# The first modulation read in eight pieces, S5's parameters moved behind it, and five reads on another queue

## The chip, the cores and the metric

One core of a Trainium2 chip runs the whole program. Its engines are TensorE (PE; PEld is its weight load), VectorE (DVE), ScalarE (ACT) and GpSimd (POOL); SyncE (SP) issues transfers, and so do ACT and POOL on queues of their own. The metric is the device time of one execution in microseconds; lower is better.

## What is computed

The reference is a trunk of two layers on 512 latent and 256 context tokens of width 1024. What matters here is the start of layer 0:

```python
mod = jax.nn.silu(c) @ w_mod + b_mod            # [1024] @ [1024, 6144], for c and for c_ctx
sh1, sc1, ... = jnp.split(mod, 6)
proj = (x * (1.0 + sc1) + sh1) @ w_in           # the operand of the projection, then the projection
pr, ps, pq, pk, pv = jnp.split(proj, ...)       # inputs of RWKV, S5 and attention
# S5: a complex state space model; its parameters come from lam_re, lam_im and log_dt
dt = jnp.exp(log_dt)[:, None]
mag = jnp.exp(lam_re * dt)
ab_re, ab_im = mag * jnp.cos(lam_im * dt), mag * jnp.sin(lam_im * dt)
```

Behind it follow the three mixers, the output product, a mixture of 32 experts, and the second layer in the same way.

## The kernel before, in words

`trunk` (L2099) runs the stages in order; the change touches the first stage of layer 0 (L2124 to L2152), and the next one, `input_side` (L2055), takes over its results.

**First stage.** `mod_c` (L91) reads `c` and `c_ctx`, applies silu, and reads `b_mod` in columns. `s5_params` (L1001) computes the table `s_pk` (powers of the discretised states, for both layers and directions) out of three small parameters. Its five reads go out on ACT's queue (L1010, L1015); two transposes bring lambda to the layout needed (L1017), and some 150 VectorE instructions, nearly all on 128 x 64 elements, do the rest; at the end `s_pk` is stored by SP (L1093). `win` (L214) reads a 256-column piece of `w_in` and splits it into two float32r parts (ACT L225, VectorE L226). `mod_unit` (L114) takes `n` columns of `w_mod`: a read on SP (L118), 16 matmul pieces for the 8 row groups (L127), an eviction on ACT (L129), small matmuls that fold and transpose it (L135), and an addition on VectorE into the columns of shift and scale (L136). It is called for 512 columns of shift and 512 of scale, twice over (`h`), with two buffers. `turn` reads the six 128-row tiles of ctx and x on ACT's queue (L2140, three buffers), and `x_turn` (L148) transposes them on PE; ACT and VectorE evict them into `xr` in turns (L154). `x_split` (L157) does one of 8 slices of the operand: scale and shift (ACT L165; VectorE L163 for every fourth), a cast into `xT[0]` (L166) and the remainder into `xT[1]` (L167; odd slices on POOL). A slice needs all six tiles and the shift and scale of its columns. `s5_bc` (L1105) reads and transposes S5's B and C.

**Second stage.** `input_side` projects. PE's order in it is the written one: tiles 8 and 9 (S5's input `uF`) first, then the steps of `s5` (L1230), with tiles of the projection (`proj` L230, matmuls L243) put in between by the list `TILES`, then the remaining tiles. An S5 step makes tables out of `s_pk`, B and C (`s5_turns` L1203, `s5_tables` L1137, first instruction L1150), sums them on PE (L1334), scans on VectorE (L1343) and multiplies by the tables again (L1280).

**What sets the order.** The order in the file is the order of priority, and a scheduler fixes, when the kernel is built, one sequence for every engine and queue from it and from its own idea of when inputs are there. On the chip each engine keeps to its sequence: an instruction that waits holds back what stands behind it. Where a buffer is to be written again, the read that fills it waits for its readers.

Of the kernel before, what the change touches and what calls it, by code (L numbers as in the profile page):

```python
# [61 lines left out]
def row(ap):  # L62

    return ap.rearrange("(o n) -> o n", o=1)
# [49 lines left out]
def mod_unit(k, l, mp, c0, n, bufs=2):  # L114

    nc = k.nc
    wt = mp.tile([128, 8, n], F32, name='wmod', bufs=bufs)
    nc.sync.dma_start(wt, k.a['w_mod'][l].rearrange("(p k) n -> p k n", k=8)[:, :, c0:c0 + n])  # L118
    v, f = c0 // 1024, c0 % 512
    if v >= 2 and f == 0:  # L120
        k.mrow = mp.tile([2, 512], F32, name='mrow', bufs=1)
        nc.scalar.dma_start(k.mrow, row(k.a['b_mod'][l, c0:c0 + 512]).to_broadcast([2, 512]))
    b = k.bank()
    p = b[:, 0:n]
    for kk in range(8):
        g = kk % 4
        nc.tensor.matmul(p[32 * g:32 * g + 32, :], k.cc[:, kk, :], wt[:, kk, :], start=kk < 4, stop=kk >= 4, tile_position=(0, 32 * g))  # L127
    r = mp.tile([128, n], F32, name='mres', bufs=bufs)
    nc.scalar.copy(r, p)  # L129
    p2 = b[:, n:] if n < 512 else k.bank()  # L130
    if v < 2:
        cols, bc = k.cols[l]
        j0, m = c0 // 128, n // 128
        for j in range(m):
            nc.tensor.matmul(p2[:, 2 * j:2 * j + 2], r[:, 128 * j:128 * j + 128], k.sel, start=True, stop=True)  # L135
        nc.vector.scalar_tensor_tensor(cols[:, v, j0 % 8:j0 % 8 + m, :], p2[:, 0:2 * m].rearrange("p (j s) -> p j s", s=2), float(v),  # L136
                                       bc[:, j0:j0 + m, None].to_broadcast([128, m, 2]), op0=ALU.add, op1=ALU.add)
        return
    nc.tensor.matmul(p2[0:2, 0:n], k.sel, r, start=True, stop=True)
    o = k.mrow[:, f:f + n]  # L140
    nc.vector.scalar_tensor_tensor(o, p2[0:2, 0:n], 1.0 if v == 4 else 0.0, o, op0=ALU.add, op1=ALU.add)
    if f + n == 512:
        nc.scalar.dma_start(k.dram('modrow%d' % l, [2, 4, 1024])[:, v - 2, c0 % 1024 - f:c0 % 1024 + n], k.mrow)
# [857 lines left out]
def s5_params(k, P, Z):  # L1001

    nc, a = k.nc, k.a
    V, A, G = nc.vector, nc.scalar, nc.gpsimd
    N = 64
    pk = Z.tile([128, 44, N], F32, name='s_pk')
    ar, ai, ais, rc, rs, m8, cr, cs = pk[:, 0:9], pk[:, 9:18], pk[:, 18:27], pk[:, 27:34], pk[:, 34:41], pk[:, 41], pk[:, 42], pk[:, 43]
    z = {}
    dt = P.tile([128, N], F32, name='s_dt')
    A.dma_start(dt, row(a['s5_log_dt'].rearrange("l d g -> (l d g)")).to_broadcast([128, N]))  # L1010
    exp_exact(k, P, dt, dt, N)
    for n in ('re', 'im'):
        t = P.tile([N, 2, 64], F32, name='s_ln' + n)
        for h in range(2):
            A.dma_start(t[:, h, :], a['s5_lam_' + n].rearrange("l d g p -> (l d g) p"))  # L1015
        p = k.bank()
        tr(k, p[:, 0:N], t.rearrange("g h p -> g (h p)"))  # L1017
        z[n] = P.tile([128, N], F32, name='s_l' + n)
        A.copy(z[n], p[:, 0:N])

    def new(n, w=N):
        return P.tile([128, w], F32, name=n)

    def mul(o, x, y):
        V.tensor_tensor(o, x, y, op=ALU.mult)

    mag, r, q = new('s_mag'), new('s_r'), new('s_q')
    mul(mag, z['re'], dt)
    exp_exact(k, P, mag, mag, N)

    mul(r, z['im'], dt)
    V.tensor_scalar(q, r, 0.15915494309189535, MAGIC, op0=ALU.mult, op1=ALU.add)
    V.tensor_scalar(q, q, -MAGIC, None, op0=ALU.add)
    for c in (-6.28125, -1.9340515136718750e-3, -1.2556659146741148e-6):
        V.scalar_tensor_tensor(r, q, c, r, op0=ALU.mult, op1=ALU.add)
    V.tensor_scalar(r, r, 3.14159, -3.14159, op0=ALU.min, op1=ALU.max)

    ph = P.tile([128, 2, N], F32, name='s_ph')
    A.activation(ph[:, 1], r, AF.Sin)
    A.activation(ph[:, 0], r, AF.Sin, scale=0.5)  # L1040
    mul(ph[:, 0], ph[:, 0], ph[:, 0])
    V.tensor_scalar(ph[:, 0], ph[:, 0], -2.0, 1.0, op0=ALU.mult, op1=ALU.add)

    V.memset(ar[:, 0], 1.0)
    V.memset(ai[:, 0], 0.0)
    mul(ar[:, 1], mag, ph[:, 0])
    mul(ai[:, 1], mag, ph[:, 1])

    def cmul(o_r, o_i, x_r, x_i, y_r, y_i, t):
        mul(o_r, x_r, y_r)  # L1050
        mul(t, x_i, y_i)
        V.tensor_tensor(o_r, o_r, t, op=ALU.subtract)
        mul(o_i, x_r, y_i)
        mul(t, x_i, y_r)
        V.tensor_tensor(o_i, o_i, t, op=ALU.add)

    t4 = P.tile([128, 4, N], F32, name='s_t4')
    for n in (1, 2, 4):
        b = [128, n, N]
        cmul(ar[:, n + 1:2 * n + 1], ai[:, n + 1:2 * n + 1], ar[:, 1:n + 1], ai[:, 1:n + 1],  # L1060
             ar[:, n:n + 1].to_broadcast(b), ai[:, n:n + 1].to_broadcast(b), t4[:, 0:n])

    c0, s0 = ph[:, 0], ph[:, 1]
    for n in range(9):
        if n < 2:
            c1, s1 = new('s_c%d' % n), new('s_s%d' % n)
        else:
            c1, s1 = rc[:, n - 2], rs[:, n - 2]
        cmul(c1, s1, c0, s0, c0, s0, t4[:, 0])
        c0, s0 = c1, s1  # L1070
    V.tensor_scalar(rs, rs, k.sgn[:, 0:1], None, op0=ALU.mult)
    mul(m8, mag, mag)
    mul(m8, m8, m8)
    mul(m8, m8, m8)

    ci, den, t = new('s_ci'), new('s_den'), new('s_t')
    mul(den, z['re'], z['re'])
    mul(t, z['im'], z['im'])
    V.tensor_tensor(den, den, t, op=ALU.add)
    V.reciprocal(den, den)  # L1080
    nr = new('s_nr')
    V.tensor_scalar(nr, ar[:, 1], -1.0, None, op0=ALU.add)
    mul(cr, nr, z['re'])
    mul(t, ai[:, 1], z['im'])
    V.tensor_tensor(cr, cr, t, op=ALU.add)
    mul(cr, cr, den)
    mul(ci, ai[:, 1], z['re'])
    mul(t, nr, z['im'])
    V.tensor_tensor(ci, ci, t, op=ALU.subtract)
    mul(ci, ci, den)  # L1090
    V.tensor_scalar(cs, ci, k.nsgn[:, 0:1], None, op0=ALU.mult)
    V.tensor_scalar(ais, ai, k.nsgn[:, 0:1], None, op0=ALU.mult)
    nc.sync.dma_start(k.dram('s5pk', [128, 44, 32]), pk[:, :, 32:64])  # L1093
    return pk
# [134 lines left out]

def s5(k, l, P, pk, BC, uF, yd):  # L1230

# [3 lines left out]
    emit_ctx = l == 0  # L1235
    z = s5_z(s5_pk(k, l, P, pk), *(BC or s5_bc(k, l, P)))
    gw = P.tile([128, 2, 256], F32, name='s_gw')
# [816 lines left out]

def input_side(k, l, W, pk, BC, xT, uF):  # L2055

    nc = k.nc
    dr = {n: k.dram(n + str(l), s) for n, s in (('cvd', [6, 128, 8, 128]), ('qd', [6, 128, 4, 128]), ('kvd', [128, 2, T]), ('yd', [6, 128, 8, 128]))}
    with ExitStack() as st:
# [14 lines left out]
        with k.tc.manual_schedule(engines={ET.PE}):  # L2074
# [6 lines left out]
            k.stream = ('s', 4)  # L2081
            for n, step in enumerate(s5(k, l, S, pk, BC, uF, dr['yd'])):
                if n == 0 and l == 0:
# [15 lines left out]
def trunk(tc, a, out):  # L2099
    k = K(tc, a)  # L2100
    nc = k.nc
    with ExitStack() as st:
# [7 lines left out]
        def psum(s):  # L2110
            k.ps = k.pool('ps', s, space=PSUM)
# [9 lines left out]
        Z = k.pool('s5pk', sZ)  # L2121
        W = k.pool('win', sX, side='right')
        uF = None
        with ExitStack() as s1:  # L2124
            psum(s1)
            k.stream = ('m', 5)
            mod_c(k)
            z = k.pool('z', s1)
            xr = z.tile([128, 8, T], F32, name='xr')
            with ExitStack() as s2:  # L2130
                mp = k.pool('mod', s2)
                k.stream = ('x', 3)
                pk = s5_params(k, k.pool('s5t', s2), Z)
                win(k, 0, W, 4)
                k.stream = ('m', 5)
                def turn(n):
                    k.stream = ('x', 3)
                    for i in n:
                        x = z.tile([128, D], F32, name='x', bufs=3)
                        nc.scalar.dma_start(x, x_in(i))  # L2140
                        x_turn(k, xr, i, x)

                for h in range(2):
                    k.stream = ('m', 5)
                    for c0 in (512 * h, 1024 + 512 * h):
                        mod_unit(k, 0, mp, c0, 512)
                    if h == 0:
                        turn(range(6))
                    for kk in range(4 * h, 4 * h + 4):
                        x_split(k, 0, xT, xr, kk)  # L2150
                k.stream = ('x', 3)
                BC = s5_bc(k, 0, Z)  # L2152
        for l in range(2):
            NTOK = T if l == 0 else LT
            hd, yb, x1 = k.dram('hd%d' % l, [NTOK, D]), k.dram('yb%d' % l, [3072, 512]), k.dram('x1_%d' % l, [NTOK, D])
            with ExitStack() as s1:
                psum(s1)
                dr = input_side(k, l, W, pk, BC, xT, uF)
            sX.close()
            sZ.close()  # L2160
            BC = None
            sP, sC, sA = ExitStack(), ExitStack(), ExitStack()
# [3 lines left out]
            with ExitStack() as s1:  # L2166
                mp = k.pool('mod', s1)
# [116 lines left out]
```

## Time and profile before

| | us |
|---|---|
| median of three runs (2838.5 to 2843.27) | 2841.53 |
| the profiled execution, its own time | 2848.87 |
| its span, first to last instruction | 2847.1 |
| PE busy in the span | 2222.6 (78%) |
| VectorE busy | 1165.4 (41%) |
| ScalarE busy | 517.5 (18%) |
| GpSimd busy | 805.1 (28%) |

The span is one execution as the hardware profiler took it; the runs are timed without it. Busy shares are means over stages with different limits, so the first 265 us have to be read by themselves. A timeline row gives start, duration, engine, line, operation, output and input tile, and in brackets for how long its engine had sat idle and what ended that.

### The profile page before, as it was taken

The page shows a single profiled execution, that of the slowest core. Times are in us where ns is not written, and L with a number is a line of the kernel's source. Part 1 is how long each engine was busy: PE and PEld are TensorE (multiplying, and loading weights), DVE is VectorE, ACT ScalarE, POOL GpSimd, SP SyncE. Part 2 cuts the span into 40 slices and gives each one's busy share as a digit, 9 for nine tenths or more (in the row PEclk, how much of TensorE's full clock was granted, in tenths as well). Part 3 has the DMA queues.
Part 4 walks back from the last instruction along what each step waited for, and adds up shares of the span by engine and source line. Part 5 has one row for each costly group of instructions (what it writes and reads, how often), then busy time and mean ns, then how long its engine had stood idle before and what let it go on. Part 6 is the DMA issues. An engine that isn't in the chain of part 4 may idle for free. (4 is left out here: it accounts for less than half of the span.)

```text
span 2847.1 us, 43425 instructions
## 1 busy us (share of the span) xinstructions
PE 2222.6 (78%) x16189; PEld 1485.8 (52%) x16189; DVE 1165.4 (41%) x2836; ACT 517.5 (18%) x1264; POOL 805.1 (28%) x1160
## 2 busy tenths in 40 slices
PE   5898677888973978999856788787797397888882
PEld 3787455666542544555525676565554254454441
DVE  7972556563384000101026873656545611111113
ACT  3222333222010000101015122333120100000001
POOL 2651534330152111101016653434334210111002
PEclk8999788598986999999987898688798698999996
DMA  8334567665547899989974325556774799989994
GB/s 243 95 95 118 152 189 200 173 183 172 191 172 239 347 416 368 392 336 375 380 280 117 82 57 148 134 143 162 217 226 155 229 378 417 419 348 367 376 421 185
DMA packets 413931, 690.01 MB, mean 242 GB/s; under 512 B 148882, under 2 KB 318610, under 8 KB 397232
## 3 DMA queue, kind: packets, MB, share of 16 engines
q1 hardware_dynamic: 310368, 594.85, 58.7%
q10 hardware_dynamic: 74960, 56.54, 6.8%
q0 software_dynamic: 28288, 34.32, 3.7%
q8 instruction: 210, 3.44, 0.5%
q14 instruction: 105, 0.86, 0.1%
HBM read 606.46 MB, written 95.47 MB: 247 GB/s over the span
## 5 line engine op out<-in xcount | busy, mean ns | idle before, releaser
L1776 PE MATMUL b_m<-w,xT 128*64 128x256 f32 x4928 | 596.2, 398 | 128.4 <-DMA w<-in_expert_w_gate_dram 80.4
L1776 PEld LDWEIGHTS b_m<-w,xT 128*64 128x64 f32 x4928 | 391.8, 143 | 335.2 <-issue 148.1
L243 PE MATMUL b_m<-xT,win 128*128 128x256 f32 (+1 forms) x1416 | 275.9, 355 | 8.5 <-POOL xT L167 3.7
L243 PEld LDWEIGHTS b_m<-xT,win 128*128 128x128 f32 x1416 | 232.6, 201 | 42.6 <-POOL xT L167 4.5
L1800 PE MATMUL b_m<-w,aT 128*64 128x512 f32 x1024 | 230.9, 592 | 1.1 <-issue 0.6
L1789 DVE COPY aT<-b_m 128x256 f32<-128x256 f32 x64 | 27.2, 425 | 475.2 <-PE b_m L59 475.2
L1806 POOL DMA_INDIRECT yb<-y,dx x64 | 63.9, 998 | 427.7 <-DVEq L1921 257.1
L1800 PEld LDWEIGHTS b_m<-w,aT 128*64 128x64 f32 x1024 | 75.5, 137 | 118.0 <-issue 108.8
L876 PE MATMUL b_a<-kz,qb 128*128 128x128 f32 (+2 forms) x416 | 116.4, 424 | 17.1 <-ACT pr L897 12.7
L1778 ACT ACTIVATE act<-b_m 128x256 f32<-128x256 f32 x64 | 24.5, 383 | 577.6 <-PE b_m L1776 565.9
L1779 DVE TENSOR_TENSOR act<-act,b_m 128x256 f32<-128x256 f32 x64 | 27.0, 421 | 233.6 <-PE b_m L1776 233.6
L1602 PE MATMUL b_a<-wo,yt 128*128 128x512 f32 x240 | 112.7, 614 | 0.0
L876 PEld LDWEIGHTS b_a<-kz,qb 128*128 128x128 f32 x416 | 79.0, 237 | 43.5 <-ACT pr L897 15.4
L127 PE MATMUL b_a<-wmod,cc 128*32 128x128 f32 x1280 | 69.0, 325 | 33.6 <-DMA wmod<-in_w_mod_dram 29.7
L1806 POOL DMA_INDIRECT yb<-yo,dx x13 | 12.9, 995 | 289.6 <-ACTq L1921 146.7
L59 PE MATMUL b_a<-idf,pr 128*128 128x128 f32 x320 | 59.4, 311 | 27.5 <-ACT pr L897 9.9
L656 POOL TENSOR_TENSOR sn<-st,gc 128x128 f32<-128x128 f32 x44 | 25.1, 570 | 182.2 <-DVE st L647 168.4
L1869 POOL DMA_INDIRECT xg<-hd,ix x32 | 33.0, 1030 | 152.8 <-PE b_m L59 122.7
L1602 PEld LDWEIGHTS b_a<-wo,yt 128*128 128x128 f32 x240 | 44.0, 193 | 47.4 <-issue 46.0
L127 PEld LDWEIGHTS b_a<-wmod,cc 128*32 128x32 f32 x1280 | 40.5, 125 | 53.6 <-DMA wmod<-in_w_mod_dram 20.4
L551 POOL TENSOR_TENSOR tl<-Bm,Xh 112x4 f32<-112x4 f32 (+13 forms) x112 | 38.6, 344 | 90.6 <-DVE Xh L552 43.5
L503 PE MATMUL b_g<-ar,bz 128*128 128x128 f32 (+1 forms) x384 | 61.0, 322 | 3.8 <-ACT bz L495 3.8
(536 smaller groups left out, 3965.0 us busy)
## 6 DMA issues: line engine op xcount, KB each, us to landing
w<-in_expert_w_gate_dram SPq DMA_DIRECT2D x64, 2048.0 KB
w<-in_expert_w_up_dram SPq DMA_DIRECT2D x64, 2048.0 KB
w<-in_expert_w_down_dram SPq DMA_DIRECT2D x64, 2048.0 KB
wmod<-in_w_mod_dram SPq DMA_DIRECT2D x80, 512.0 KB
rec<-rec SPq DMA_DIRECT2D x40, 512.0 KB
win<-in_w_in_dram SPq DMA_DIRECT2D x16, 1024.0 KB
wmod<-in_w_mod_dram SPq DMA_DIRECT2D x4, 2048.0 KB
sca<-sc SPq DMA_DIRECT2D x24, 256.0 KB
```

The costliest lines, as they stand in the source:

```text
L59: k.nc.tensor.transpose(out, x, k.idf[r:r + n, r:r + n])
L127: nc.tensor.matmul(p[32 * g:32 * g + 32, :], k.cc[:, kk, :], wt[:, kk, :], start=kk < 4, stop=kk >= 4, tile_position=(0, 32 * g))
L243: nc.tensor.matmul(p[:, :n], wt[u][:, kk, j * 128:j * 128 + 128], xT[v][:, kk, c0:c0 + n], start=kk == 0 and q == 0, stop=kk == 7 and q == 2)
L503: nc.tensor.matmul(pv[:, cp, q, 0:n, :], bk[:, hp, q, cp].rearrange("p s t -> p (s t)"), ar[:, 0:n, cp, q, :], start=True, stop=True)
L551: eng.tensor_tensor(t[:, 0:n, j:32], Bm[:, r0:r1, j:j + 1].to_broadcast([112, n, w]), x.to_broadcast([112, n, w]), op=ALU.mult)
L876: nc.tensor.matmul(dst, qb[:, 2 * v + e, :], kz[:, v, r, 128 * keys[c][0]:128 * keys[f - 1][0] + 128], start=c == 0 or (c == 4 and r == 0) ...
L1602: nc.tensor.matmul(ps[h], y[:, kt, :], wo[:, kt, 512 * h:512 * h + 512], start=kt == 0, stop=kt == 5)
L1776: mm = nc.tensor.matmul(p[64 * h:64 * h + 64, 0:256], xT[:, kk, :], w[:, kk, 256 * h:256 * h + 256], start=kk == 0, stop=kk == 7)
L1789: k.nc.vector.tensor_copy(aT, pa[:, 0:256].rearrange("p (j x) -> p j x", j=2))
L1800: nc.tensor.matmul(py[64 * s:64 * s + 64, :], aT[:, j, 64 * h:64 * h + 64], wd[:, q, 512 * s:512 * s + 512], start=q == 0, stop=q == 3)
L1806: sc = nc.gpsimd.indirect_dma_start(out=yb, out_offset=bass.IndirectOffsetOnAxis(ap=dst, axis=0), in_=y, in_offset=None, bounds_check=3071 ...
L1869: return nc.gpsimd.indirect_dma_start(out=out, out_offset=None, in_=hd, in_offset=bass.IndirectOffsetOnAxis(ap=idx, axis=0), bounds_check= ...
```

## The change

The eight pieces: `mod_unit` is called with 256 columns and four buffers, four rounds of shift and scale, and each round is followed by two slices of the operand instead of four. The second product of a unit then goes into the free half of the bank of the first (L130). `s5_params` and its pool move from the head of the stage to behind the last slice, ahead of `s5_bc`. Its five reads go to POOL's queue.

```diff
@@ s5_params
-    A.dma_start(dt, row(a['s5_log_dt'].rearrange("l d g -> (l d g)")).to_broadcast([128, N]))
+    G.dma_start(dt, row(a['s5_log_dt'].rearrange("l d g -> (l d g)")).to_broadcast([128, N]))
...
-            A.dma_start(t[:, h, :], a['s5_lam_' + n].rearrange("l d g p -> (l d g) p"))
+            G.dma_start(t[:, h, :], a['s5_lam_' + n].rearrange("l d g p -> (l d g) p"))
@@ trunk
                 mp = k.pool('mod', s2)
-                k.stream = ('x', 3)
-                pk = s5_params(k, k.pool('s5t', s2), Z)
                 win(k, 0, W, 4)
-                k.stream = ('m', 5)
                 def turn(n):
...
-                for h in range(2):
+                for h in range(4):
                     k.stream = ('m', 5)
-                    for c0 in (512 * h, 1024 + 512 * h):
-                        mod_unit(k, 0, mp, c0, 512)
+                    for c0 in (256 * h, 1024 + 256 * h):
+                        mod_unit(k, 0, mp, c0, 256, 4)
                     if h == 0:
                         turn(range(6))
-                    for kk in range(4 * h, 4 * h + 4):
+                    for kk in range(2 * h, 2 * h + 2):
                         x_split(k, 0, xT, xr, kk)
                 k.stream = ('x', 3)
+
+                pk = s5_params(k, k.pool('s5t', s2), Z)
                 BC = s5_bc(k, 0, Z)
```

## Rows read from the trace of the kernel before

**Rows 1.** Stretches: from:to, length, busy (count) by engine, clock, DMA share, GB/s
```profile
0.00:10.96 10.96, 0.00 (x0) 0.00 (x0) 1.16 (x16) 0.00 (x0) 2.62 (x18) 1.00 0.72 130
10.96:61.57 50.61, 30.73 (x173) 17.99 (x174) 46.71 (x195) 19.32 (x33) 8.21 (x5) 0.86 0.90 287
61.57:131.00 69.43, 58.31 (x347) 50.05 (x347) 62.63 (x152) 16.97 (x25) 45.22 (x59) 0.91 0.38 98
131.00:190.00 59.00, 58.14 (x396) 52.65 (x397) 52.00 (x135) 15.48 (x24) 38.97 (x58) 0.97 0.32 83
```

**Rows 2.** Timeline of the issuing queues, ACT's, then SP's
```profile
2.99 2.52 ACTq L1010 DMA_DIRECT2D s_dt<-in_s_log_dt_dram  x1
...
10.96 0.35 ACTq L2140 DMA_DIRECT2D x<-in_ctx_dram  x1
...
5.66 0.69 SPq L118 DMA_DIRECT2D wmod<-in_w_mod_dram  x1
...
13.18 0.55 SPq L118 DMA_DIRECT2D wmod<-in_w_mod_dram  x1
...
34.54 0.54 SPq L118 DMA_DIRECT2D wmod<-in_w_mod_dram  x1
```

**Rows 3.** Waits of SP's queue, 0 to 36 us: total, times, longest
```profile
SPq L118 <- DMA s_lnre<-in_s_lam_re_dram: 6.8, 1, 6.8
```

**Rows 4.** Stretches again, cut by the DMA rate (last column)
```profile
10.00:34.30 24.30, 14.58 (x82) 8.65 (x82) 19.51 (x104) 7.53 (x13) 0.00 (x0) 0.93 1.03 388
34.30:36.00 1.70, 1.70 (x18) 1.46 (x15) 1.70 (x9) 1.13 (x2) 0.00 (x0) 1.00 0.21 60
6.00:42.30 36.30, 19.71 (x122) 11.77 (x122) 27.51 (x147) 11.37 (x20) 0.00 (x0) 0.95 0.97 351
77.00:78.00 1.00, 1.00 (x6) 0.84 (x5) 1.00 (x4) 0.00 (x0) 0.00 (x0) 1.00 1.08 386
```

**Rows 5.** Timelines of several engines, from the last product to dense projection
```profile
43.58 1.08 PE L127 MATMUL b_m<-wmod,cc 128*32 128x512 f32 x4 [3.40 <-DMA wmod<-in_w_mod_dram]
...
47.27 0.58 ACT L129 COPY mres<-b_m 128x512 f32<-128x512 f32 x1 [3.39 <-PE b_m L127]
...
51.45 0.16 DVE L136 SCALAR_TENSOR_TENSOR cols<-b_m,bmc 128x8 f32<-128x8 f32 x1
...
59.09 2.17 POOL L167 TENSOR_TENSOR xT<-xr,xT 128x768 fp32r<-128x768 f32 x1
...
61.31 17.21 PE L243 MATMUL b_m<-xT,win 128*128 128x256 f32 x74 [0.67 <-POOL xT L167]
```

**Rows 6.** Timeline of VectorE: first parameter, first constant, first table
```profile
10.96 0.20 DVE L976 TENSOR_SCALAR xe_r<-s_dt 128x64 f32<-128x64 f32 x1 [8.72 <-DMA s_dt<-in_s_log_dt_dram]
...
15.58 0.22 DVE L75 TENSOR_SCALAR tri<-jp 128x128 bf16<-128x128 f32 x1
...
61.57 0.21 DVE L1150 TENSOR_TENSOR s_bb<-s_b,s_pk 128x64 f32<-128x64 f32 x1
```

**Rows 7.** Timeline of PE in the first S5 steps
```profile
83.38 0.88 PE L59 MATMUL b_s<-idf,s_ut 96*128 96x96 f32 x8 [3.98 <-ACT s_ut L1313]
...
86.44 3.01 PE L1334 MATMUL b_s<-s_uT,s_em 128*128 128x96 f32 x16
...
123.97 0.46 PE L1280 MATMUL b_y<-s_l,s_GC 128*96 128x128 f32 x2 [2.70 <-DVE s_GC L1351]
...
130.98 1.10 PE L1334 MATMUL b_s<-s_uT,s_em 128*128 128x96 f32 x8 [1.89 <-DVE s_em L1176]
```

**Rows 8.** Line L2072, POOL's store of kvd: issue in ns, landing
```profile
L2072 POOL DMA_DIRECT2D kvd<-qs x8: 539/550/809, 257.1 to 1746.3; - x8
...
DMA to landing us min/median/max: 2.8/2.9/3.0
```

**Rows 9.** DMA issues: KB of each, median us to landing
```profile
rec<-av POOLq DMA_DIRECT2D x24, 128.0 KB, 8.1
```

**Rows 10.** VectorE, ACT and POOL on tile xr alone, columns as in rows 1
```profile
10.96:61.57 50.61, 14.41 (x20) 12.45 (x20) 7.89 (x4) 0.86 0.90 287
```

## The prediction

> **What bounds the kernel now.** I read busy time by stretch first [rows 1], then the queues and the DMA rate [rows 2 to 4], then the timelines of the engines in the two stretches the change can touch [rows 5 to 7].
>
> The profiled execution spans 2847.1 us and took 2848.9 us; the median of the three runs is 2841.5, so 7.4 us lie between the two. I work out a difference on the profiled execution and apply it to the median. A difference under about 0.2% (5.7 us) can't be told from none.
>
> The change sits before 61.57 us, where layer 0's first S5 table starts. Up to there PE is busy 30.7 of 50.6 us and VectorE 46.7. From 61.57 to 131 PE has 58.3 of 69.4 and VectorE 62.6, and from 131 to 190 PE has 58.1 of 59.0 [rows 1]. So the start is VectorE's, the first S5 steps belong to PE and VectorE in turns, and from 131 us PE is full with projection. What arrives early before 61 us gains only if S5's steps up to 131 follow, because PE executes projection and S5 in one written order.
>
> **Part 1, the reads on Pool's queue.** Before, ACT's queue spends 2.52 us issuing `s_dt`, and the first `x` read is issued at 10.96 us, in the very moment in which `s_dt` has landed and VectorE, idle for 8.72 us, starts on it [rows 2, 6]. On SP the second w_mod read goes out only at 13.18, after 6.8 us of waiting that the profile ends by the landing of `s_lnre` [rows 2, 3]. So slow small reads hold back large ones. After, ACT issues two `b_mod` reads and then `x`, near 3 us, and SP does not meet the lambda reads. Pool issues the five reads instead. One issue on Pool costs 0.54 to 0.81 us, and from issue to landing it is 2.9 us for the store of `kvd`, 8.1 for that of `rec` [rows 8, 9]. Pool's start-up work ends by about 3 us (2.62 us busy [rows 1]), so `s_dt` lands between 6 and 12 us. The bulk reads leave SP from 5.66 us on [rows 2], behind these small ones, so the shorter row is the nearer: I take 7.5, a gain of 3.5 us on 10.96, with ends of +5 and -1. The 2.7 to 4.1 us of issues lie on an idle Pool. Queued behind them on Pool is nothing before the first xT subtract, which is far later; if Pool's cover were gone, those 4 us would be the price.
>
> In the stretch in which this happens the trace has VectorE busy for 1.16 us of 10.96 [rows 1]. The Trainium skill (SBUF — State Buffer, "SBUF: two separate sides") speaks against this part: Pool builds its descriptors in software, through ports that certain VectorE instructions lock, so a read on its queue can starve behind VectorE. By it the five reads would lose what VectorE holds there, at most that 1.16 us; no run so far shows it.
>
> **Part 2, eight reads of 1 MB and four buffers.** The bytes are the same. DMA moves 388 GB/s from 10 to 34.3 us, falls to 60 from 34.3 to 36.0 because the last w_mod read is issued only at 34.54, when a buffer is free, and averages 351 from 6 to 42.3 [rows 2, 4]. 36.3 us x 351 / 388 = 32.8, so with reads always outstanding DMA is done at 38.8 instead of 42.3. The pieces become 1 KB per row instead of 2 KB; a w_in read of such pieces runs at 386 [rows 4], so I take no loss. The last product starts at 43.58, 1.3 us behind the DMA's end [rows 5]; after, at 38.8 + 1.3 = 40.1. Ends: 43.6 (nothing gained) and 40.1.
>
> That the rate holds is read from one row. The Trainium skill (DMA: Bandwidth & Descriptors, "Bandwidth") has a rule against smaller reads: a 1 MB read reaches 341 GB/s, 16 MB 425. By it 8.4 MB would take an estimated 24.6 us instead of 21.6, and the last piece would come 3 us later. The 386 of the lone w_in read, also 1 MB, disagrees in its middle microsecond.
>
> Added instructions: four more evictions on ACT, bounded by 0.58 us each [rows 5], ACT being busy 19.3 of 50.6; four more column adds on VectorE at 0.16, 0.6 us in all; more but narrower products on PE, which has 20 us to spare [rows 1]. The second product now goes into the other half of the same bank: it waited for the eviction before too, so nothing.
>
> **The tail of the operand.** From the last product's start (43.58 us) to dense projection (61.31) it is 17.7 us [rows 5]. Of it 3.7 is product up to the eviction, 4.2 eviction to the last column add (VectorE has S5's instructions in front), 9.9 splitting four slices of the operand. After: product of half the width 1.9, eviction, selection and add 1.6, two slices instead of four 4.5 (half of 9.9 is 4.9; the Pool subtract alone is 2.17), so 8.0. Projection turns dense at 48 instead of 61.3: **13 us earlier on PE**.
>
> **Part 3, S5's parameters behind.** This decides how much of 13 us counts. Of VectorE's 46.7 us up to 61.57, 14.4 work on `xr` [rows 10]; some 25 to 30 are parameters and constants. They do not shrink, they move behind the operand where both are ready. VectorE keeps a fixed order: at 10.96 it sat for 8.7 us before `s_dt` although `tri`, which needs no DMA, was ready and ran at 15.58 [rows 6]. So an operand instruction placed ahead of its data now idles VectorE. I take the same work plus 0.6, from 7.5 us, with 4 us of idle time (before: 3.9): 7.5 + 47.3 + 4 = 58.8 for the first table, **2.8 us earlier** than 61.57. Ends: 53 (start at 6, no idle) and 75 (all parameters, at least 25 us, behind the operand at 48, and 2 more: the first table stands 2.5 us behind the start of the operand's last subtract, 59.09 [rows 5, 6]).
>
> The store of `s_pk` on SP moves with the parameters, ahead of the next w_in read; that read feeds a tile that PE reaches after the first scan, and PE gets there no sooner than the tables, so nothing.
>
> **Sum.** PE waits for tables after projecting u: of 13 us it loses about 10. VectorE's start moves by -2.8. In the steps up to 131 PE's waits on VectorE (2.70 at 123.97, 1.89 at 130.98 [rows 7]) stay, since VectorE sets them; the 3.98 before 83.38, where ACT sits behind a weight read, shrinks as u comes early, and I count 1.5 of it. Behind 131 PE is full, everything shifts. -2.8 - 1.5 = **-4.3 us**: 2844.6 for the profiled execution, 2837.2 for the median. From there I assume a pure shift, since the later stages are untouched.
>
> **Rivals.**
> 1. *S5 does not hold PE back* (faster). If the parameters fit wholly into waits before 48 us, tables start at 53 to 55.5, and PE, which is ahead, never has to wait in the first steps, the gain is -7.6 to -12.5 (8.5 of the start, 4 of waits): 2829 to 2834. For: VectorE has idle time before 11 us. Against: it is busy 46.7 of the 50.6 after. Chance 0.26.
> 2. *The parameters come late* (slower). Place: VectorE's queue between the first column add and the last operand subtract. If operand instructions stand early in the fixed order and wait for DMA, the parameters are left for after 48 us. Each microsecond left there goes onto the start of the tables: 48 + left + 2. It decides from left = 11.6, where the start is 61.6 as before; 15 us give 65, +3.4; 20 give 70, +8.4 (2850); all 25 give +13. For: the 8.7 us wait; the 2.7 to 4.1 us of issues before the last lambda lands. Against: of the 40 us from 7.5 to 48 the operand takes 14.4, which leaves room for over 20 us of parameters. Chance of more than +5.7: 0.19; what stays below counts with rival 3.
> 3. *Reads of half the size are slower, or Pool's come at 12 us:* operand 3 us later, still under the tables' start; -1 to +1, 2841. Or the change does not do what it says, since the order on the engines comes out as before: 0. Chance 0.13.
>
> **How the numbers follow.** The forecast's own case (start between 55.5 and 63, -7.6 to 0; 2834 to 2842) has 0.42. The 80% range reaches into both rivals: 2828 to 2850. Faster by over 5.7 us: rival 1 whole, 0.26, and 0.11 of the forecast's case, 0.37. Slower: rival 2, 0.19. Same: the rest, 0.44.
>
> **What would show it.** `x` issued before 5 us and DMA without a dip near 34 us (part 1, 2); last w_mod product at 40.1 and dense projection at 48 (tail); the first table at 58.8 and VectorE's waits before the operand under 5 us (part 3); PE idle for some 10 us between u and the first S5 scan, which stood at 86.44 [rows 7]. A first table later than 62 us with a long VectorE wait for column adds or `x` makes me wrong on the side of rival 2; a first table before 55.5 on that of rival 1.

## The result, and the profile after

The changed kernel takes **2859.53 us** (median of six runs, 2850.34 to 2863.07) against 2841.93 for the kernel before beside it: ratio 1.006, 95% interval 1.0041 to 1.008, or 11.7 to 22.7 us more. The prediction was 2837.2 with a range of 2828 to 2850: wrong, and on the side of the prediction's rival 2.

The profiled execution of after took 2850.34 us, the lowest of the six, over a span of 2848.5; that of before took 2848.87. So the loss isn't read from the two spans. It is read from the first 300 us: there two executions of one kernel agree closely (the control below), and further on they don't. I match every instruction of one trace with its twin in the other and take the median difference of their starts; from 100 to 290 us the changed kernel stands **10.5 us** behind before.

First the stretches of after, with their length, busy time and count of PE, PEld, DVE, ACT and POOL, then granted clock, DMA share and GB/s:

```profile
0.00:10.96 10.96, 0.00 (x0) 0.00 (x0) 4.09 (x36) 1.50 (x2) 5.58 (x23) 1.00 0.82 120
10.96:61.57 50.61, 34.12 (x245) 23.30 (x246) 36.34 (x125) 19.11 (x36) 7.64 (x5) 0.76 0.97 299
61.57:131.00 69.43, 51.48 (x315) 44.48 (x313) 64.84 (x192) 15.05 (x23) 42.92 (x57) 0.85 0.38 85
131.00:190.00 59.00, 54.68 (x352) 49.61 (x353) 50.77 (x128) 13.21 (x23) 37.04 (x52) 0.88 0.32 83
```

Against [rows 1] VectorE lost 10.4 us of work between 10.96 and 61.57 (36.34 busy, 46.71 before) and gained 2.9 ahead of it; PE does 3.4 more there and 6.8 less in the next stretch. The lower clock in the last two rows (0.85 and 0.88, before 0.91 and 0.97) adds nothing behind 131 us: read 10.5 us later, from 141.5 to 200.5, after has PE busy for 58.14 us at 0.96, as before from 131 to 190 (58.14 at 0.97). VectorE's timeline in after shows where that work went:

```profile
5.17 0.17 DVE L103 TENSOR_SCALAR pm<-pm 128x8 f32<-128x8 f32 x1
15.88 2.29 DVE L226 TENSOR_TENSOR win<-win,win 128x2048 fp32r<-128x2048 f32 x1 [10.55 <-ACT win L225]
...
21.58 0.16 DVE L136 SCALAR_TENSOR_TENSOR cols<-b_m,bmc 128x4 f32<-128x4 f32 x1 [2.73 <-ACT xr L154]
...
22.29 0.18 DVE L976 TENSOR_SCALAR xe_r<-s_dt 128x64 f32<-128x64 f32 x1
...
56.74 2.60 DVE L167 TENSOR_TENSOR xT<-xr,xT 128x768 fp32r<-128x768 f32 x1
...
70.36 0.45 DVE L1071 TENSOR_SCALAR s_pk<-s_pk,sgn 128x448 f32<-128x448 f32 x1
70.75 0.22 DVE L1150 TENSOR_TENSOR s_bb<-s_b,s_pk 128x64 f32<-128x64 f32 x1
```

The constants are done at 5.3 us. Then the subtract of the first input weight heads the queue and waits 10.55 us for ScalarE's cast. The first parameter starts at 22.29 (10.96 in [rows 6]), though its input has long been there: the POOL queue's issue of `s_dt`, and what the listing of DMA issues says of it (KB, median us to landing), are

```profile
2.32 0.80 POOL L1010 DMA_DIRECT2D s_dt<-in_s_log_dt_dram  x1
3.12 1.11 POOL L1015 DMA_DIRECT2D s_lnre<-in_s_lam_re_dram  x2
4.20 1.06 POOL L1015 DMA_DIRECT2D s_lnim<-in_s_lam_im_dram  x2
```

```profile
s_dt<-in_s_log_dt_dram POOLq DMA_DIRECT2D x1, 32.0 KB, 5.2
s_lnre<-in_s_lam_re_dram POOLq DMA_DIRECT2D x2, 16.0 KB, 7.3
```

so it landed at 7.5 us. Of the 145 parameter instructions, 55 had started by 30 us before and 14 after; 65 of them start behind the operand's last subtract (56.74 us), none before. They end at 70.8, and the first table follows at once, 9.2 us later than in [rows 6]. PE meets that in S5's first steps. Its timeline, from the products of the modulation on:

```profile
29.14 1.07 PE L127 MATMUL b_m<-wmod,cc 128*32 128x256 f32 x16
...
34.15 1.93 PE L127 MATMUL b_m<-wmod,cc 128*32 128x256 f32 x16
...
50.02 1.93 PE L127 MATMUL b_m<-wmod,cc 128*32 128x256 f32 x16
...
59.40 14.66 PE L243 MATMUL b_m<-xT,win 128*128 128x256 f32 x77 [1.22 <-DVE xT L167]
...
84.49 1.11 PE L59 MATMUL b_s<-idf,s_ep 128*128 128x128 f32 x4 [6.34 <-POOL s_ep L1168]
...
87.66 1.44 PE L1334 MATMUL b_s<-s_uT,s_em 128*128 128x96 f32 x8
96.84 1.99 PE L1334 MATMUL b_s<-s_uT,s_em 128*128 128x96 f32 x8 [7.74 <-DVE s_K L1198]
```

By a scan I mean, as the prediction does, the products on PE (L1334) that VectorE then scans. The first one starts 1.2 us later than in [rows 7], its second half waits 7.74 us for the tables, and the second scan stands at 106.3 instead of 95.9. The wait of 6.34 us is not VectorE's alone: POOL's L1168, which ends it, took 5.19 us from 79.25 on, beside VectorE's work, and 1.47 before, at 69.81. The DMA rates, cut as in [rows 4], are

```profile
12.00:18.00 6.00, 2.58 (x11) 2.12 (x11) 2.12 (x1) 2.48 (x2) 0.00 (x0) 1.00 1.07 376
18.00:24.00 6.00, 3.94 (x36) 2.58 (x40) 3.01 (x13) 1.45 (x3) 0.00 (x0) 1.00 1.06 368
24.00:30.00 6.00, 4.37 (x53) 2.92 (x45) 3.18 (x10) 2.15 (x5) 0.00 (x0) 1.00 1.08 369
30.00:36.00 6.00, 3.79 (x34) 2.23 (x30) 3.40 (x15) 2.86 (x6) 0.00 (x0) 0.81 1.08 353
42.30:46.00 3.70, 3.21 (x25) 1.67 (x28) 3.70 (x20) 0.40 (x2) 0.57 (x1) 0.50 0.54 75
6.00:42.30 36.30, 18.64 (x154) 12.34 (x158) 17.56 (x50) 13.35 (x23) 3.21 (x3) 0.88 1.09 345
```

The dip near 34 us is gone, yet the mean to 42.3 us is 345 GB/s where it was 351, and only from there on does the rate fall off.

### The profile page after: what moved, and what is told of

Its sections match the earlier page's. It is cut to its first block, busy times and chain, and to the rows that moved or that the text cites. A ratio compares the mean times of both kernels' runs of the same rounds, so it can differ in the third digit from the quotient of the medians.

```text
span 2848.5 us, 43581 instructions
## 1 busy us (share of the span) xinstructions
PE 2210.2 (78%) x16253; PEld 1484.1 (52%) x16253; DVE 1168.2 (41%) x2840; ACT 518.7 (18%) x1268; POOL 811.6 (28%) x1165
## 5 line engine op out<-in xcount | busy, mean ns | idle before, releaser
L876 PE MATMUL b_a<-kz,qb 128*128 128x128 f32 (+2 forms) x416 | 111.7, 411 | 17.4 <-ACT pr L897 12.0
L127 PEld LDWEIGHTS b_a<-wmod,cc 128*32 128x32 f32 x1280 | 40.1, 124 | 51.7 <-DMA wmod<-in_w_mod_dram 17.3
L883 DVE TENSOR_REDUCE mx<-b_a 128x1 f32<-128x512 f32 (+1 forms) x80 | 48.5, 630 | 30.8 <-PE b_a L882 23.3
```

The costliest lines, as they stand in the source:

```text
L876: nc.tensor.matmul(dst, qb[:, 2 * v + e, :], kz[:, v, r, 128 * keys[c][0]:128 * keys[f - 1][0] + 128], start=c == 0 or (c == 4 and r == 0) ...
L883: V.tensor_reduce(mx[:, 0, r:r + 1], aa[r][:, 0:w], axis=AX.X, op=ALU.max)
```

## The experiments

The three parts are called A (the reads on POOL's queue), B (eight pieces, four buffers) and C (the parameters behind the operand). In the kernel's own terms three theories stood at the start: theory 1, C leaves too much of the parameters for the end; rival 2, A makes VectorE stand behind the weight's subtract; rival 3, B chains eight pieces through PE and ACT. These numbers are not the prediction's: its rival 2 is theory 1 here. From A alone on, each expectation says itself what its theory 1 is. The table gathers all runs; times are of the one profiled execution, in us, and an instruction's is its start.

| kernel | ratio to before, 95% interval | VectorE busy + idle to the table | first table | operand's last subtract | u's last product | second scan | shift at 140 to 280 |
|---|---|---|---|---|---|---|---|
| before | | 47.9 + 13.7 | 61.6 | 59.1 | 78.1 | 95.9 | |
| before again | 0.9989 [0.9968, 1.001] | 47.9 + 13.9 | 61.8 | 59.3 | 77.9 | 96.3 | +0.1 |
| after (A, B, C) | 1.006 [1.0041, 1.008] | 49.3 + 21.5 | 70.8 | 56.7 | 73.7 | 106.3 | +10.5 |
| A, B | 1.003 [1.0007, 1.0053] | 47.6 + 21.0 | 68.7 | 67.9 | 86.8 | 106.5 | +9.5 |
| B, C | 1.0085 [1.0056, 1.0115] | 50.0 + 26.1 | 76.1 | 57.9 | 76.8 | 109.7 | +14.0 |
| A, C | 1.0029 [1.0008, 1.005] | 49.2 + 21.5 | 70.7 | 62.9 | 79.8 | 106.2 | +10.7 |
| C | 1.0045 [1.0023, 1.0067] | 51.9 + 25.1 | 77.0 | 63.5 | 81.5 | 109.7 | +13.2 |
| A | 1.0015 [0.9993, 1.0037] | 47.0 + 19.0 | 66.0 | 65.2 | 84.1 | 102.6 | +6.7 |
| B | 1.0022 [1.0002, 1.0041] | 46.7 + 15.6 | 62.3 | 61.9 | 80.1 | 100.2 | +4.9 |
| after, subtract on POOL | 1.0056 [1.0034, 1.0078] | 53.8 + 21.4 | 75.1 | 58.6 | 76.0 | 108.4 | +12.6 |
| A, B, subtract on POOL | 1.0037 [1.0017, 1.0057] | 45.3 + 21.7 | 67.0 | 66.2 | 84.9 | 104.8 | +9.2 |
| A, cast and subtract on POOL | 1.0014 [0.9991, 1.0036] | 51.0 + 14.4 | 65.4 | 64.6 | 84.0 | 102.2 | +5.5 |
| cast and subtract on POOL | 1.0004 [0.9983, 1.0025] | 50.4 + 17.8 | 68.2 | 65.4 | 83.9 | 104.2 | +8.3 |
| A, both on POOL, next weight early | 1.0017 [0.9994, 1.0041] | 51.3 + 13.7 | 65.0 | 66.7 | 84.5 | 101.6 | +5.7 |
| A, weight later | 1.0023 [1.0001, 1.0046] | 47.2 + 20.5 | 67.7 | 66.8 | 85.9 | 104.0 | +7.3 |
| after, weight later | 1.0063 [1.0035, 1.0091] | 50.6 + 28.6 | 79.2 | 59.9 | 76.9 | 112.9 | +17.4 |
| weight later | 1.0006 [0.9982, 1.0031] | 46.3 + 12.5 | 58.8 | 58.4 | 76.0 | 96.0 | -0.2 |
| A, B, weight later | 1.0039 [1.0016, 1.0062] | 45.6 + 22.5 | 68.1 | 69.8 | 86.6 | 106.2 | +9.5 |
| weight later, next weight early | 1.0015 [0.9996, 1.0035] | 50.1 + 13.3 | 63.4 | 60.7 | 80.3 | 95.4 | -0.3 |

**The control.** The kernel before, run once more.

> The kernel before once more, unchanged, as the control. All theories: the first four layers' instructions stand within 0.5 us of the first profiled execution up to 280 us, so that a shift of 5 us there is a property of a kernel's order and not of an execution; behind 300 us instructions may stand some us apart; the ratio's interval holds 1.

From 60 to 290 us the median shift of every stretch of 10 us is within 0.4 us of the first execution (0.7 ahead of that, and single instructions stand up to 1.7 us apart), so a shift of 5 us there belongs to the kernel. From 300 us on the same two traces drift between -5.5 and +4.6 us, and the expectation named that too. A small difference of total times is therefore weak evidence and the shift the better one. Over the 18 rows with both, the two go together (correlation 0.83). And in every row the second scan's delay against before is the shift within 1.1 us: whatever holds that scan sets what follows.

**C undone (A and B stay).**

```diff
+                k.stream = ('x', 3)
+                pk = s5_params(k, k.pool('s5t', s2), Z)
                 win(k, 0, W, 4)
+                k.stream = ('m', 5)
...
-                pk = s5_params(k, k.pool('s5t', s2), Z)
```

> Eight reads and four buffers and Pool's reads kept, s5_params put back to the head of the stage. In the order fixed at build time none of the 147 parameter instructions on VectorE stands behind the operand's last subtract (65 do in the changed kernel). Theory 1 (the parameters behind the operand delay the first S5 table): first table at 58 to 63 us instead of 70.75, PE's shift at 200 us from +10.5 down to -4 to +2, time within 6 us of before. Rival 2 (the reads on Pool's queue cost it, since VectorE now stands behind the weight subtract until 16 us): first table near 66, shift +5, time +5 to +8. Rival 3 (the split into eight pieces costs it, the operand being chained through PE and ACT): dense projection no earlier than 59, shift +10, time +12 to +17 as in the changed kernel.

Theory 1 fell in the form in which it stood: with the parameters ahead of the operand again the shift is +9.5, near rival 3's +10. VectorE's waits to 80 us (total, times, longest):

```profile
DVE win L226 <- ACT win L225: 9.1, 1, 9.1
DVE xr L154 <- PE b_x L59: 5.3, 5, 2.2
DVE s_den L1025 <- ACT s_lre L1019: 3.6, 1, 3.6
```

The 9.1 us behind the weight is rival 2's, but now it is the operand that comes late (last subtract 67.9, u's last product 86.8). So there are two gates, the tables and u, and VectorE's idle time pays for whichever its order puts last. I formed a second theory from that: VectorE's busy time up to the first table is nearly the same in every order (45 to 54 us in all runs, with what holds it below), and the shift comes from the idle time its order lets in.

**A undone (B and C stay).**

```diff
-    G.dma_start(dt, ...
+    A.dma_start(dt, ...
...
-            G.dma_start(t[:, h, :], ...
+            A.dma_start(t[:, h, :], ...
```

> The changed kernel with the five reads back on ACT's queue. 74 parameter instructions stand behind the operand. Theory 1: first table at 70 or later, shift at 200 us +9 to +13, time +10 to +20. Rival 2 (Pool's reads): first table at 62 or earlier, shift under +3. Rival 3 (eight pieces): as the changed kernel.

Worse, +14.0: behind the `x` reads on ACT's queue the small reads leave late, and VectorE waits 9.2 us for x copies, 7.1 for the weight and 7.0 for the columns. Rival 2, by which the table should have come at 62 or earlier, falls here: within the changed kernel A was a help.

**B undone (A and C stay).**

```diff
-                for h in range(4):
+                for h in range(2):
...
-                    for c0 in (256 * h, 1024 + 256 * h):
-                        mod_unit(k, 0, mp, c0, 256, 4)
+                    for c0 in (512 * h, 1024 + 512 * h):
+                        mod_unit(k, 0, mp, c0, 512)
...
-                    for kk in range(2 * h, 2 * h + 2):
+                    for kk in range(4 * h, 4 * h + 4):
```

> The changed kernel with four pieces of 512 columns and two buffers as before. 37 parameter instructions stand behind the operand instead of 65. Theory 1: in between, first table at 64 to 68, shift at 200 us +3 to +7, time +3 to +10. Rival 3 (eight pieces): shift 0, time as before. Rival 2: shift +5 whatever the order.

The table comes at 70.7 and the shift is +10.7, as with B. All three theories miss that: theory 1 had 64 to 68 for the table, as only 37 parameters stand behind the operand instead of 65, so their number alone doesn't set it. The pieces bring the operand's last subtract forward by 6.2 us (56.7 against 62.9) and change nothing behind, since the tables are the gate.

**C alone.** The kernel before with `s5_params` behind the last slice.

> Before with one part of the change, s5_params behind the last slice; four pieces, reads on ACT's queue. 63 parameter instructions stand behind the operand. Theory 1: first table at 68 to 73, shift at 200 us +7 to +12, time +7 to +17. Rivals 2 and 3: neither part is in it, so first table near 61.6 and time as before.

+13.2 without the other two parts, more than theory 1 had, so C alone is enough to lose. VectorE's waits in it:

```profile
DVE xr L154 <- PE b_x L59: 10.1, 4, 8.6
DVE win L226 <- ACT win L225: 6.6, 1, 6.6
DVE cols L136 <- PE b_m L135: 4.6, 4, 2.7
```

**A alone and B alone**, each put on the kernel before by its hunk of the diff.

> The kernel before with only the five reads of the parameters moved to GpSimd's queue. Theory 1: the reads alone put VectorE's queue behind the weight subtract, first parameter at 16 us or later, idle time of VectorE before the first table near 20 us instead of 13.7, the table at 65 to 68 us, the shift after it +5 to +9.5. Rival (the reads on GpSimd's queue are harmless, what hurt with them was the eight pieces): first parameter near 8 us, table at 58 to 61, shift -3 to 0.

> The kernel before with only the modulation in eight parts of 256 columns and four buffers. Theory 1 (the pieces are not what is lost): the first parameter at 11 us as before, the table at 60 to 63, the shift after it -3 to +2, the time within 0.3% of before. Rival 3 (eight pieces, chained through TensorE and ScalarE, hold the operand and ScalarE's work for the parameters): the operand's last subtract at 62 us or later, the table at 65 or later, the shift +5 to +10.

A alone hits the second theory's numbers (first parameter 17.9, idle 19.0, table 66.0, shift +6.7). VectorE's longest wait in it:

```profile
DVE win L226 <- ACT win L225: 10.2, 1, 10.2
```

B alone misses both: the table is nearly in place (62.3), and still the shift is +4.9, more than the +2 allowed. What carries it is a third gate. ScalarE's cast of the third input weight stands ahead of u's last copy; in B its timeline reads

```profile
83.56 1.90 ACT L225 CAST win<-win 128x2048 fp32r<-128x2048 f32 x1 [8.14 <-DMA win<-in_w_in_dram]
85.36 0.58 ACT L2051 COPY uF<-b_m 128x512 f32<-128x512 f32 x1
```

where before has the cast at 79.98. The read of that weight stands on SP behind two stores of S5's tables (from 72.89 before, from 76.17 here), so a later table delays u as well. The tables are later than their start tells: the first instruction took 1.80 us in B, beside a subtract on POOL (the lock shown below), and 0.21 before [rows 6]. The parts don't add up: 6.7, 4.9 and 13.2 alone make 24.8, and all three together 10.5.

**The wait behind the weight taken away by moving its subtract to POOL**, in the changed kernel and with A and B:

```diff
-        (nc.gpsimd if at in (1, 3) else nc.vector).tensor_tensor(w[1], ...
+        (nc.gpsimd if at in (1, 3) or (l, at) == (0, 4) else nc.vector).tensor_tensor(w[1], ...
```

> The changed kernel, whole, with one instruction moved: the subtract of the first input weight's second bf16 term (line 226, 2.3 us) goes from VectorE to GpSimd. Theory 1 (VectorE's time lost at the head of the kernel: in the changed kernel that subtract heads VectorE's queue for 10.5 us, until ScalarE has cast the weight at 15.9 us): the first parameter starts near 12 us instead of 22.3, the first table is ready at 60 to 65 us instead of 70.8, the work after it stands +0 to +5 us against before instead of +10.5, and the time falls below the changed kernel's by 5 us or more. Rival A (the parameters that stand behind the operand's last subtract are the loss by themselves): the first table stays at 69 us or later and the shift at +9 or more. Rival B (the wait only moves to the next instruction that wants a late input, the x0 copies): the first parameter starts near 16 us, the table near 67, the shift +6 to +8.

> The reads on GpSimd's queue, eight pieces, the parameters ahead of the operand as before, and the weight subtract on GpSimd. Theory 1: no wait of VectorE longer than 4 us is left before 20 us, the first table at 55 to 60 us, the shift after it -6 to -2 us, the first four layers' time at or below before. Rival B (the x0 copies wait in its place): first parameter near 16, table near 65, shift +4 to +8. Rival C (the operand, late behind the parameters, takes over): table at 60 or earlier, but the operand's last subtract at 65 us or later and the shift +5 to +8.

Theory 1 came true in neither. In the changed kernel the wait moved to the next late input, as its rival B said, but the table came at 75.1 where that rival had 67, with a shift of +12.6; these two numbers are rival A's, by which the parameters behind the operand are the loss. VectorE's longest wait there, in front of the x copies, is the last number:

```profile
DVE xr L154 <- PE b_x L59: 17.8, 3, 10.4
```

(Another part of that loss is the lock shown next, in which the first parameter took 3.98 us.) With A and B the parameters start at 7.3 us, as hoped, and stop at once, 11.2 us long (`s_den` on ScalarE's copy of lambda, behind the weight's cast and, on PE, behind the first product of the modulation).

**Cast and subtract on POOL**, with A, alone, and with A and the next weight's read ahead of S5's b and c reads (the subtract's line is as above, the reads' as in A):

```diff
-        nc.scalar.copy(w[0], r)
+        (nc.gpsimd.tensor_copy if (l, at) == (0, 4) else nc.scalar.copy)(w[0], r)
...
+                win(k, 0, W, 5, load=True)
                 k.stream = ('x', 3)
                 BC = s5_bc(k, 0, Z)
```

> The kernel before with the five reads on GpSimd's queue, and the cast and the subtract of the first input weight (lines 225 and 226) on GpSimd too, so that neither VectorE nor ScalarE stands behind that weight's read. Theory 1 (what the reads cost was that wait: 10.2 us at line 226 in the run with the reads alone): the first parameter starts near 7.5 us, the lambda copies on ScalarE are done by 13 us, the first table at 55 to 59 us, the operand's last subtract at 56 to 60, the shift after it -4 to 0 us. Rival (another wait takes its place, on the x copies or on TensorE): table at 62 or later, or last subtract at 63 or later, and a shift of +4 or more.

> The kernel before, its reads as they were, with only the cast and the subtract of the first input weight on GpSimd. Theory 1: the parameters still start at 11 us; VectorE and ScalarE are free of 2.3 and 1.9 us of work, so the table and the operand come 0 to 2 us earlier, the shift -2 to +1 us, the time within 0.2% of before. If it gains as much as the run with the reads moved too, the earlier reads are worth nothing.

> As the run with reads and weight on GpSimd, and the second input weight's read issued ahead of S5's b and c reads (one line in the head), so that its cast on ScalarE no longer stands between the copies of u. Theory 1: u is ready 1 to 3 us earlier than in that run, the shift -6 to -2 us, the time at or below before. Rival: the third weight's cast, which waits for a buffer, still stands ahead of u's last copy, and the shift is that run's within 1 us.

With A the idle time is down to 14.4 us and the start at 7.3, and the table is still late. VectorE's timeline in that run, and POOL's beside it:

```profile
12.15 1.88 DVE L988 TENSOR_SCALAR xe_p<-xe_p 128x64 f32<-128x64 f32 x1
14.06 0.22 DVE L987 TENSOR_TENSOR xe_p<-xe_p,xe_r 128x64 f32<-128x64 f32 x1
14.32 0.22 DVE L988 TENSOR_SCALAR xe_p<-xe_p 128x64 f32<-128x64 f32 x1
14.57 4.47 DVE L987 TENSOR_TENSOR xe_p<-xe_p,xe_r 128x64 f32<-128x64 f32 x1
```

```profile
12.07 1.91 POOL L225 CAST win<-win 128x2048 fp32r<-128x2048 f32 x1 [6.82 <-DMA win<-in_w_in_dram]
...
14.46 4.50 POOL L226 TENSOR_TENSOR win<-win,win 128x2048 fp32r<-128x2048 f32 x1
```

An instruction that takes 0.22 us took 4.47, as long as POOL's subtract ran (4.50, ended 0.08 us earlier); another took 1.88 beside POOL's cast. Together 5.9 us of standing still count as busy. So these runs swapped a wait for a lock and couldn't tell what the wait alone is worth. Without A the same lock took 4.79 us and the shift was +8.3, where -2 to +1 had been expected; VectorE's idle time grew by 4.1 us as well, in front of column adds and an x copy. The early read of the next weight moved nothing (+5.7 against +5.5), as its rival said.

**The weight later**, with cast and subtract on their old engines: its line goes behind the first turn of x.

```diff
-                win(k, 0, W, 4)
...
                     if h == 0:
                         turn(range(6))
+                        win(k, 0, W, 4)
```

> The kernel before with the five reads on GpSimd's queue and the line that reads and splits the first input weight moved behind the first turn of x, so that its subtract stands at place 162 of VectorE's queue instead of 35. Theory 1 (the reads lose only by the wait behind that subtract): first parameter near 7.5 us, VectorE idle 10 to 13 us before the table's first instruction instead of 19, the table at 57 to 61 us, the shift behind it -4 to +1 us. Rival (the operand takes over: its last subtract at 62 us or later): the shift +3 or more though the table is early.

> The changed kernel, whole, with the same line moved behind the first turn of x. Theory 1 (the weight's wait is most of the loss): the table at 61 to 65 us instead of 70.8, the shift -2 to +4 us instead of +10.5. Rival A (the loss is the parameters' place: VectorE has nothing but the x path to do while x and the modulation weight come in): VectorE still idle 18 us or more before the table, the table at 67 us or later, the shift +7 or more.

> The kernel before with only that line moved. Theory 1: first parameter at 11 us as before, table at 60 to 63 us, shift -2 to +2 us; the difference to the run with the reads moved too is what the reads on GpSimd's queue are worth once nothing stands ahead of the parameters: 2 to 4 us by theory 1, none by the rival that the operand sets the end.

> The reads on GpSimd's queue, the eight pieces, the parameters ahead of the operand and that line moved. Theory 1: first parameter near 7.5 us, table at 58 to 63, shift -3 to +3. Rival 3 (eight pieces keep the operand back): last subtract at 64 us or later, shift +4 to +8.

The changed kernel got worse by this (+17.4), so its rival A holds and the second theory's "most of the loss is the weight's wait" falls. VectorE's waits there:

```profile
DVE xr L154 <- PE b_x L59: 12.4, 6, 3.9
DVE cols L136 <- PE b_m L135: 11.6, 6, 8.4
DVE xe_r L976 <- DMA s_dt<-in_s_log_dt_dram: 2.1, 1, 2.1
```

Parameters start at 7.6 us, but only 21 of them have started by 30 us; the first wait for columns alone is 8.4 us. With A alone the wait moved as well, to lambda. PE's timeline in that run begins:

```profile
20.03 1.88 PE L127 MATMUL b_m<-wmod,cc 128*32 128x512 f32 x2 [20.03 <-DMA wmod<-in_w_mod_dram]
21.84 0.37 PE L59 MATMUL b_x<-idf,s_lnre 64*128 64x64 f32 x1
```

The small transposes, whose reads land near 11 us by the times of after, stand behind a product that needs the first 2 MB, and VectorE waits 10.4 us for them. With A and B, too, the later weight moves the wait, to the column adds (8.1 us the longest): the table comes at 68.1, the operand's last subtract at 69.8 as its rival 3 had it, and the shift stays at +9.5. Only with neither A nor C does the later weight help: table 58.8, last subtract 58.4, u's last product 76.0, all earlier than before by 0.7 to 2.8 us, though the first table instruction then takes 1.80 us beside POOL, which leaves 1.2 of the 2.8. The shift is -0.2, as expected, and the third weight's cast still stands at 79.86. The last run adds one line to this one, to take that wait away:

```diff
+                win(k, 0, W, 5, load=True)
                 k.stream = ('x', 3)
                 BC = s5_bc(k, 0, Z)
```

> The kernel before with the first input weight's line behind the first turn of x and the second weight's read ahead of S5's b and c reads, which lets the third weight's read go out near 60 us instead of 74. Theory 1 (ScalarE's wait for the third weight at 71 to 80 us is what holds u once it is computed): that wait falls to 5 us or less, u's last copy starts at 78 to 79.5 instead of 81.7, the first scan at 83 to 85.5, the shift -3.5 to -1 us, the time within 0.2% of before or below. Rival (the tables or VectorE behind them hold the second scan anyway): the first scan is earlier, but the second and the shift stay within 1 us of before.

ScalarE's timeline in it, at the same place as in B above:

```profile
80.51 1.90 ACT L225 CAST win<-win 128x2048 fp32r<-128x2048 f32 x1 [4.87 <-PE b_m L243]
82.31 0.58 ACT L2051 COPY uF<-b_m 128x512 f32<-128x512 f32 x1
```

The weight is there, and the cast now waits for PE to be done with the buffer that it writes, which is u's last product; the second weight's cast and subtract now stand ahead of the operand's end, at 48.07 and 54.40 us (u's last product 80.3). The shift is -0.3, and its rival was right. No version of these beats before by what can be measured.

**What the runs together say.** Shown: without A and C VectorE idles 12 to 16 us before the first table (18 where POOL holds the weight), with either of them 19 to 29, save the two runs with A that lost the time to the lock instead. In the order of before the parameters fill the time in which x and w_mod come in (55 started by 30 us before, 14 in the changed kernel, 5 with C alone). C takes just that filling away: in all six kernels with C VectorE's first long wait ends at 12 to 17 us, and removing one such wait uncovered the next. Behind the operand's end, at 59.3 us, 10.8 us of parameters remain in the changed kernel (6 to 14 in the others with C). Not shown: that the 7 us between the shift (10.5) and the medians' difference (17.6) come from the same cause; nor what each of A, B and C has of the 10.5, since they don't add up. The interval's lower end, 11.7, lies close to the shift, and what lies behind 300 us drifts by as much in the control.

## Why the prediction was wrong, point by point

- **Part 1, `s_dt` at 7.5 us: right, and worth nothing.** It landed at 2.32 + 5.2 = 7.5, which is partly luck, as it was to be issued near 3 and to land by a row of 2.9; `x` was issued at 3.14. The large reads gained nothing by it: to 10.96 us DMA moved 120 GB/s, 130 before. The step from there, "VectorE's start moves by -2.8", failed: the first parameter started at 22.29, because the fixed order put the weight's subtract, a column add and two x copies ahead of it. I had looked for what the reads wait for, not for what the new order puts ahead of their readers.
- **The Trainium skill's rule on reads from POOL's queue** (SBUF — State Buffer, "SBUF: two separate sides") was priced at 1.16 us at most. No starving shows in after: the five issues took 0.52 to 0.80 us each (0.54 to 0.81 in [rows 8]) beside VectorE's constants, of which after has 4.09 us there.
- **Part 2, DMA done at 38.8: wrong by the rate.** "The 386 of the lone w_in read" was a window of one microsecond. Pieces of 1 MB ran at 353 to 376 GB/s here, where the 2 MB reads of before had 388, so the dip's gain was given back and the bulk still ended near 42 us. B alone has the same rates (360 to 375), and A with C, in reads of 2 MB, 394 and 396 from 12 to 24 us, though 365 from 24 to 30; whether the size or the shorter row counts isn't shown. The Trainium skill (DMA: Bandwidth & Descriptors, "Bandwidth") says that 1 MB reads move less per second; the trace agrees in sign, with 3 to 9% (376 and 353 against 388, 1 MB against 2) where its 20% is for 1 MB against 16.
- **The tail, last product 40.1 and projection dense at 48: wrong.** 50.02 and 59.40. From the last product to dense projection it was 9.4 us, near the 8.0 of the sum. What failed is the product's start: from 34.15 us on five products follow each other at 3.4 to 4.7 us, each 1.93 of matmul, an eviction to wait for, and 1.01 of selection. I had costed the four more units at nothing on PE ("20 us to spare"), but in PE's fixed order they form a chain. The clock has a part in it: from 34 to 53 us PE was granted 0.50, the lower level of 1.2 GHz, after 12.68 us busy of the 22 from 12 to 34; before had 0.91 there, after 14.28 busy. A product took 1.93 us at 0.50 and 1.07 at 1.00 (29.14 us), so my estimate from these rows is up to 4.3 us for the five; no run took it away.
- **Part 3, the first table at 58.8: wrong, and the step that decides.** The busy time was right: 1.2 + 47.3 predicted, 49.3 measured. "With 4 us of idle time" on top of a start at 7.5, in all 10.3 us idle, was 21.5. I had written that an operand instruction placed ahead of its data now idles VectorE, and then kept the old idle time.
- **The prediction's rival 2 was the mechanism, its price too low.** It named VectorE's queue and the wait for column adds or x, and the profile shows both. At 48 us 16.6 us of parameters were left; 48 + 16.6 + 2 gives 66.6, and the table came at 70.75, since the operand itself lasted to 59.3. Of that, 1.65 us is the lock again: its last subtract took 2.60 us beside one on POOL, and 0.95 alone. With a chance of 0.19 it was the least likely of the three larger cases. The argument against it, room for over 20 us of parameters from 7.5 to 48, counted time and not readiness: 11.1 us were done.
- **The projected u did come early**, 73.7 against 78.1, and PE then lost it and more than the sum said: 6.34 and 7.74 us of waits for tables. The 3.98 us ahead of it shrank as well, to 2.33, near the 1.5 counted, and that bought nothing, since PE then waited for the tables all the same.
- **"PE is full behind 131, everything shifts"** holds to 290 us. Further on no single execution can show it.

## What to carry to other kernels

Work with small early inputs was worth most here where large inputs are still coming in; moved behind them it left an engine idle and was paid for later, even if the total of work is unchanged. Where one fixed sequence per engine is made from a scheduler's guess of arrivals, a change of queue reorders consumers that it doesn't touch, so read which instruction heads each queue and when its input lands. And before a wait is removed, look up which one stands behind it: seven of these kernels took the wait for the weight away from VectorE; five met another of 8 to 11 us, and two a lock.

## What I had not expected of the hardware

VectorE stood still for a whole instruction of POOL: 4.47 us for a 128 x 64 product beside a 4.50 us subtract of 128 x 2048, and 3.98 to 4.79 in other runs. The same shows in the kernel before, where a 128 x 256 scaling took 1.91 us as POOL's subtract of [rows 5] ran, and 0.35 in after (VectorE's timelines, before and then after):

```profile
59.51 1.91 DVE L1128 TENSOR_SCALAR s_c<-s_c,sgn 128x256 f32<-128x256 f32 x1
```

```profile
64.72 0.35 DVE L1128 TENSOR_SCALAR s_c<-s_c,sgn 128x256 f32<-128x256 f32 x1
```

The section of the Trainium skill that I had weighed for the reads (SBUF — State Buffer, "SBUF: two separate sides") says this in its other half: the port pair that GpSimd and VectorE share is locked for a whole instruction by whoever comes first. The trace agrees; not every VectorE instruction is held, a column add (L136), which reads its first operand from a PSUM bank, took its usual 0.16 us at 50.20 in after while POOL's subtract ran from 49.85 to 51.67. I had applied it to descriptors, where nothing showed, and not to POOL's arithmetic. Such time counts as busy, not as a wait, so a list of waits doesn't contain it.
